# First block of experts listed ahead of the ranking, last two blocks added by one-hot products

## The chip, the cores and the metric

One core of one Trainium2 chip runs the whole program. The metric is the device time of one execution in microseconds (us). Before the change three runs gave a median of 2994.25 us (2991.94 to 2997.94).

## The reference, cut to what matters

Two transformer blocks run one after the other over 512 tokens, and 256 context tokens beside them in the first layer, all in float32 with a model width of 1024. The first block has two layers; each ends in a mixture of 32 experts of which every token takes two. This is the part that the change touches:

```python
def routed_experts(h, e_idx, e_w, w_gate, w_up, w_down):
    ...
    def expert_block(args):
        xblk, e = args
        return (jax.nn.silu(xblk @ w_gate[e]) * (xblk @ w_up[e])) @ w_down[e]

    yb = lax.map(expert_block, (xb, block_exp)).reshape(n_rows, d)
    return jnp.zeros((n_tok + 1, d), h.dtype).at[row_tok].add(yb * row_w[:, None])[:n_tok]

def hier_moe(h, grp_w, grp_b, exp_w, exp_b, w_gate, w_up, w_down):
    ...
    top_v, top_i = lax.top_k(e_logit, TOP_K)
    w = (g_prob * jax.nn.softmax(top_v, axis=-1)).astype(h.dtype)
    e_idx = g_idx[:, None] * EXPERTS_PER_GROUP + top_i.astype(jnp.int32)
    return routed_experts(h, e_idx, w, w_gate, w_up, w_down)
```

An expert has three matrices of 1024 by 512 floats (2 MB each), so each layer reads 201 MB of expert weights. Layer 0 routes 768 tokens, layer 1 routes 512. After layer 1 comes a final norm and the second block, whose first step is a feed-forward. With these inputs the experts 0 and 1 get 51 and 62 tokens in layer 0, 33 and 11 in layer 1.

## The kernel before

The activations X stay on chip, feature-major (8 tiles of 128 features by tokens). `moe` (L830) runs once per layer. It computes the router logits, writes the normalised tokens to a table `h2d` in DRAM (`token_major`), and then `router` (L607) picks two experts per token and gives each token its position within its expert. `places` (L663) ranks the 32 experts by load; two fixed experts (`FIRST`) always stand first, so that their weights can be loaded before the ranking is known. `order_list` (L700) writes the ranking to `pordi`; SyncE (SP) reads the expert numbers from it before it can issue the weights of any ranked expert. `slots` (L724) turns the places into lists, with one one-hot tile `sB` per 128 assignments on VectorE and one product each on TensorE: `stok` (which token sits in which row of which block), `srow` (the row of the result table) and `swt` (its weight).

The work then goes in blocks of 128 rows. A block is a single expert (the two fixed ones and the `MANY` most loaded ones: 8 in layer 0, 4 in layer 1) or a pair of lightly loaded experts with 64 rows each, which run in the two column halves of TensorE. There are 21 blocks in layer 0 and 19 in layer 1; the two fixed singles come first, then singles and pairs in turn, then pairs. `expert` (L1063) is a generator with four steps: transposes of the gathered rows, gate, up, down. For block e the program writes gate(e), the gather of block e+1 on GpSimd's queue, down(e-1) with the scatter of its weighted rows to the table `Yd` in DRAM, then up(e). Weights come through `raw` (L117) in pieces of 512 KB, 12 per expert, 384 per layer, in a ring of 24 buffers filled by SP's queue. The order of the instructions on each engine is made by a scheduler from the order of the program and its priorities.

The last block is not scattered. Its rows are added to X by products with a one-hot matrix `own` (L994 to L1012). All other rows come back from `Yd` by six (layer 0) or four (layer 1) reads `yr` of 1 MB on SP's queue, written in the program after the last block (L990); GpSimd adds the two rows of each token (L1020), TensorE transposes them (L1028, L1030), VectorE adds them to X (L1035 to L1041); squares and their sums for the next norm follow tile by tile (L1042 to L1055). In layer 1 the feed-forward (`ffn`, L1372) starts when these sums are there; `final_rows` (L1358) makes the row scales from them.

Among the rest of layer 1 are the s5 preparations (many small VectorE operations), which are spread beside the feed-forward.

Of the kernel before, what the change touches and what calls it, by code (L numbers as in the profile page):

```python
# [11 lines left out]
F32 = DT.float32  # L12
# [9 lines left out]
KD = 8  # L22
# [37 lines left out]
class Kernel:  # L60
    def __init__(self, tc, A):
        self.tc, self.nc, self.A = tc, tc.nc, A
        self.n = 0
        self.live = []
        self.fenced, self.behind, self.last_raw = 0, [], None
# [51 lines left out]
    def raw(self, src, queue=None):  # L117
# [9 lines left out]
        with ExitStack() as st:  # L127
            ins = self.behind.pop(0) if self.behind else None
            if ins:
                st.enter_context(self.tc.issue_after(ins))  # L130
# [180 lines left out]
    def open_x(self, ctx, n):  # L311
# [4 lines left out]
        self.rwc = p.tile([128, n, 36], F32, name="rwc")  # L316
        st.callback(s2.close)
# [283 lines left out]
    def router(self, l, lt, pool, p2, n_tok):  # L601
# [58 lines left out]
        V.tensor_copy(cnt, pc[:, :NE])  # L660
        self.choice = (oh, pos, v3, cnt)
        return self.places(l, p2, tt)

    def places(self, l, pool, tt):

        V = self.nc.vector
        oh, pos, _, cnt = self.choice
        mk = lambda name, *s, dt=F32: pool.tile([128, *s], dt, name="p" + name)
        n1 = FIRST[l] + MANY[l]
        nb = n1 + (NE - n1) // 2  # L670
# [17 lines left out]
        n = nb + nb % 2  # L688
        ohb = mk("ohb", tt, 2, n)
        V.tensor_tensor(ohb, self.iota[:, :n].unsqueeze(1).unsqueeze(1).to_broadcast([128, tt, 2, n]),  # L690
# [7 lines left out]
        return ohb, slot, nb  # L698

    def order_list(self, l, pool, p2):  # L700
# [12 lines left out]
        V.tensor_scalar(self.cap, self.cap, 128.0, None, op0=ALU.add)  # L713
# [10 lines left out]
    def slots(self, pool, rel, rhs, n_tok, name, bufs):  # L724
# [5 lines left out]
        n = rhs.shape[-1] // 3  # L730
        ps = self.bank()
        for t in range(tt):
            for j in range(2):
                B = pool.tile([128, 128], F32R, name=self.uid(name + "B"), tag=name + "B", bufs=bufs)
                V.tensor_scalar(B, self.iota, rel[:, t, j:j + 1], None, op0=ALU.is_equal)
                nc.tensor.matmul(ps[:, :3 * n], B, rhs[:, t, j], start=t == 0 and j == 0, stop=t == tt - 1 and j == 1)
# [3 lines left out]
        row = pool.tile([128, n], I32, name=name + "row")  # L740
        V.tensor_copy(row, f)
        tok = pool.tile([128, n], I32, name=name + "tok")
        V.tensor_scalar(tok, row, 1, None, op0=ALU.arith_shift_right)
        wt = pool.tile([128, n], F32, name=name + "wt")
# [32 lines left out]
    def overflow(self, l, n_tok, h2d, Yd, p2, x):  # L777
# [7 lines left out]
        with tc.If(nb > 0):  # L785
            with tc.For_i(0, nb, 1) as i:
                with ExitStack() as st:
# [25 lines left out]
                    row, tok, wt = self.slots(pool, rel, rhs, n_tok, "o", 2)  # L813
# [16 lines left out]
    def moe(self, l, n_tok, fg, side_work, stats):  # L830
# [8 lines left out]
        with ExitStack() as st:  # L839
# [4 lines left out]
            with ExitStack() as st1:  # L844
# [3 lines left out]
                with ExitStack() as st2:  # L848
# [36 lines left out]
                    for i in range(len(segs)):  # L885
                        for k in range(KD):
                            V.tensor_scalar(dg[:, k, i], self.ident, ga[:, k, i:i + 1], None, op0=ALU.mult)
                        for b in range(2):
# [5 lines left out]
                            nc.scalar.activation(sr[:, i, 512 * b:512 * b + 512], ps, AF.Copy)  # L894
                    put_back = []

                    def token_major():
                        for t in range(tt):
                            i = 0 if t < 4 else 1
                            for b in range(2):  # L900
# [6 lines left out]
                                if 2 * t + b < self.quick:  # L907
# [6 lines left out]
                    ohb, slot, nb = self.router(l, lt, pool, p2, n_tok)  # L914
                    v3 = self.choice[2]
                    n = ohb.shape[-1]
                    rhs = p2.tile([128, tt, 2, 3 * n], F32R, name="rhs", tag="lg")
                    for c in range(3):
                        V.tensor_tensor(rhs[:, :, :, n * c:n * c + n], ohb,
                                        v3[:, c].bitcast(F32).unsqueeze(3).to_broadcast([128, tt, 2, n]), ALU.mult)  # L920
                    row, tok, wt = self.slots(p2, slot, rhs, n_tok, "s", 2 * tt)
                    token_major()
                    self.behind = [None] * self.ahead[l] + put_back[1::2]
                    srow, stok, swt = [pool.tile([128, n], d, name=x) for x, d in (("srow", I32), ("stok", I32), ("swt", F32))]
                    for a, b in ((srow, row), (stok, tok), (swt, wt)):
                        V.tensor_copy(a, b)
                    self.order_list(l, pool, p2)

                n1 = FIRST[l] + MANY[l]
# [3 lines left out]
                ranks = lambda b: [b] if b < n1 else [2 * b - n1, 2 * b - n1 + 1]  # L933
                ysc = []
                with ExitStack() as st2:
# [26 lines left out]
                    for e in range(nb):  # L962
# [7 lines left out]
                        if e:  # L970
                            put(e - 1, self.rows_of(p2, next(ex[e - 1]), swt[:, turn[e - 1]:turn[e - 1] + 1]))
# [1262 lines left out]
```

## Time and profile before

| | us |
|---|---|
| median of 3 runs | 2994.25 |
| profiled execution, its own time | 2992.93 |
| its span in the trace | 2991.3 |
| experts of layer 0, first matmul to the scale of the next norm | 400.7 to 970.1 |
| experts of layer 1, first matmul to the feed-forward's third column block | 1324.9 to 1887.3 |

The span leaves 1.6 us of the execution's own time outside. TensorE is busy for 93% of the span, the DMA engines for between one and nine tenths of a slice, depending on the stage: in both expert stages they are at their limit for over 400 us. So the table by stretches, not the page's averages, tells which resource a stage waits for.

### The profile page before, as it was taken

The page shows a single profiled execution, that of the slowest core. Times are in us where ns is not written, and L with a number is a line of the kernel's source. Part 1 is how long each engine was busy: PE and PEld are TensorE (multiplying, and loading weights), DVE is VectorE, ACT ScalarE, POOL GpSimd, SP SyncE. Part 2 cuts the span into 40 slices and gives each one's busy share as a digit, 9 for nine tenths or more (in the row PEclk, how much of TensorE's full clock was granted, in tenths as well). Part 3 has the DMA queues.
Part 4 walks back from the last instruction along what each step waited for, and adds up shares of the span by engine and source line. Part 5 has one row for each costly group of instructions (what it writes and reads, how often), then busy time and mean ns, then how long its engine had stood idle before and what let it go on. Part 6 is the DMA issues. An engine that isn't in the chain of part 4 may idle for free.

```text
span 2991.3 us, 34947 instructions
## 1 busy us (share of the span) xinstructions
PE 2770.2 (93%) x12662; PEld 1815.0 (61%) x12662; DVE 1231.7 (41%) x2183; ACT 910.5 (30%) x1488; POOL 451.9 (15%) x430
## 2 busy tenths in 40 slices
PE   7989979998997999979999997999999889999998
PEld 3756734433433889844433333778888767888886
DVE  3883431000005566542000004954436777444335
ACT  3563201110102467511110002333225666323223
POOL 1662110000002000010100001371003140000000
PEclk9999989999998999989999998899999999999999
DMA  7558569999997211448999997343333422333331
GB/s 245 198 191 291 177 203 382 403 404 394 399 403 306 77 52 29 149 162 316 406 412 414 412 414 298 92 131 116 94 97 117 134 64 76 97 94 96 99 92 64
DMA packets 211426, 642.98 MB, mean 215 GB/s; under 512 B 32016, under 2 KB 41328, under 8 KB 209968
## 3 DMA queue, kind: packets, MB, share of 16 engines
q1 hardware_dynamic: 195648, 609.38, 56.2%
q0 software_dynamic: 15600, 31.32, 3.0%
q8 instruction: 101, 1.65, 0.2%
q14 instruction: 77, 0.63, 0.1%
HBM read 624.37 MB, written 37.19 MB: 221 GB/s over the span
## 4 chain that ended last, share of the span: by engine, by line
PE 62%; DMA 22%; DVE 9%; issue 4%; ACT 2%; SPq 1%; POOL 0%; DVEq 0%; POOLq 0%; ACTq 0%
PE ps L167 13%; PE ps L168 13%; PE ps L169 13%; PE ps L1089 9%; DMA raw<-exp_w_up 7%; DMA raw<-exp_w_down 6%; DMA raw<-exp_w_gate 6%; PE ps L1108 5%; PE ps L357 3%; DVE wl L90 1%; PE ps L1073 1%; DMA raw<-w_in_ab 1%; PE ps L219 1%; PE ps L1332 0%; DVE X L1035 0%
## 5 line engine op out<-in xcount | busy, mean ns | idle before, releaser
L1089 PE MATMUL ps<-raw,xt 128*64 128x512 f32 (+1 forms) x2048 | 635.6, 602 | 14.9 <-DMA raw<-exp_w_up 10.9
L167 PE MATMUL ps<-Hh,wh 128*128 128x512 f32 (+1 forms) x1320 | 495.5, 381 | 7.2 <-ACT Hh L260 2.1
L169 PE MATMUL ps<-Hh,wl 128*128 128x512 f32 (+1 forms) x1320 | 495.6, 377 | 6.4 <-DVE wl L90 6.3
L168 PE MATMUL ps<-Hl,wh 128*128 128x512 f32 (+1 forms) x1320 | 496.3, 377 | 1.6 <-DVE Hl L267 1.2
L1089 PEld LDWEIGHTS ps<-raw,xt 128*64 128x64 f32 (+1 forms) x2048 | 213.4, 150 | 389.6 <-issue 271.7
L88 ACT ACTIVATE wh<-raw 128x1024 fp32r<-128x1024 f32 (+1 forms) x224 | 231.5, 1039 | 559.8 <-PE ps L168 455.3
L90 DVE TENSOR_TENSOR wl<-raw,wh 128x1024 fp32r<-128x1024 f32 (+1 forms) x224 | 275.4, 1233 | 186.7 <-ACT wh L88 186.0
L1094 DVE TENSOR_TENSOR eh<-ps,eh 128x512 f32<-128x512 f32 x40 | 27.7, 692 | 753.7 <-PE ps L1089 704.8
L1108 PE MATMUL ps<-raw,ht 128*64 128x512 f32 (+1 forms) x1024 | 327.2, 603 | 2.3 <-issue 1.7
L167 PEld LDWEIGHTS ps<-Hh,wh 128*128 128x128 f32 x1320 | 248.9, 190 | 71.2 <-issue 5.6
L168 PEld LDWEIGHTS ps<-Hl,wh 128*128 128x128 f32 x1320 | 249.9, 189 | 52.5 <-issue 2.5
L169 PEld LDWEIGHTS ps<-Hh,wl 128*128 128x128 f32 x1320 | 249.1, 189 | 53.1 <-DVE wl L90 7.6
L1108 PEld LDWEIGHTS ps<-raw,ht 128*64 128x64 f32 (+1 forms) x1024 | 123.2, 150 | 192.7 <-issue 167.3
L1115 ACT ACTIVATE ey<-ps,swt 128x512 f32<-128x512 f32 x76 | 51.4, 686 | 323.8 <-PE ps L1108 305.3
L951 POOL DMA_INDIRECT yd<-ey,srow x38 | 37.9, 997 | 694.5 <-ACT ey L1115 579.5
L408 POOL TENSOR_TENSOR cg<-cg,cp 128x798 f32<-128x798 f32 x60 | 119.1, 1985 | 107.0 <-DVE cv L415 72.1
L1092 ACT ACTIVATE eh<-ps 128x512 f32<-128x512 f32 x40 | 23.9, 597 | 335.0 <-PE ps L1089 335.0
L1078 ACT ACTIVATE xt<-ps 128x512 f32<-128x512 f32 x40 | 23.9, 597 | 279.2 <-PE ps L1089 150.1
L357 PE MATMUL ps<-raw,sc 128*32 128x512 f32 x384 | 97.8, 614 | 3.5 <-DMA raw<-mod_w 3.5
L167 PE MATMUL ps<-Gh,wh 128*128 128x512 f32 x256 | 101.1, 395 | 0.0
L169 PE MATMUL ps<-Gh,wl 128*128 128x512 f32 x256 | 101.0, 395 | 0.0
L168 PE MATMUL ps<-Gl,wh 128*128 128x512 f32 x256 | 101.0, 395 | 0.0
(698 smaller groups left out, 3938.4 us busy)
## 6 DMA issues: line engine op xcount, KB each, us to landing
raw<-exp_w_up SPq DMA_DIRECT2D x256, 512.0 KB
raw<-exp_w_gate SPq DMA_DIRECT2D x256, 512.0 KB
raw<-exp_w_down SPq DMA_DIRECT2D x256, 512.0 KB
raw<-ffn_w SPq DMA_DIRECT2D x132, 512.0 KB
raw<-mod_w SPq DMA_DIRECT2D x96, 512.0 KB
yr<-yd SPq DMA_DIRECT2D x10, 1024.0 KB
X<-xT SPq DMA_DIRECT2D x16, 384.0 KB
raw<-w_in_ab SPq DMA_DIRECT2D x12, 512.0 KB
```

Source lines behind the costliest of these rows:

```text
L88: self.nc.scalar.activation(dst.hi, src, AF.Copy)
L90: self.split_last = eng.tensor_tensor(dst.lo, src, dst.hi.bitcast(F32), ALU.subtract).ins
L167: mm(ps, a.hi, b.hi, start=start, stop=False)
L168: mm(ps, a.hi, b.lo, start=False, stop=False)
L169: mm(ps, a.lo, b.hi, start=False, stop=stop)
L219: self.sums_last = self.nc.tensor.matmul(ps[:, t:t + 1], s, self.ones, start=True, stop=True).ins
L357: nc.tensor.matmul(ps[32 * g:32 * g + 32], self.sc[:, 2 * g + j, 30 - 2 * i:62 - 2 * i], w[:, j * 512:(j + 1) * 512], start=i == 0 and j = ...
L408: nc.gpsimd.tensor_tensor(a, a, t, ALU.add)
L951: ysc.append(nc.gpsimd.indirect_dma_start(out=Yd, out_offset=bass.IndirectOffsetOnAxis(ap=srow[:, b:b + 1], axis=0), in_=y, in_offset=None ...
L1089: mm(ps[s], XT[:, 2 * c + k, s], w[:, 512 * k:512 * k + 512], start=c == 0 and k == 0, stop=c == 3 and k == 1, **kw)
L1108: mm(pss[b][s], HT[:, k, s], w[:, 512 * b:512 * b + 512], start=k == 0, stop=k == 3, **kw)
L1115: self.nc.scalar.activation(y[:, 512 * b:512 * b + 512], pss[b], AF.Copy, scale=wt)
```

## The change

1. The first block is now a pair: the fixed experts 0 and 1 with 64 rows each. It has lists of its own (`fone`, `fplace`, `frhs`, `fB`, ending in `ftok`), which need only the positions and not the ranking. `places` is ordered behind them. The later blocks keep the list `s*` with the ranking. There are 20 blocks in layer 0 and 18 in layer 1, and a fixed expert's capacity falls from 128 to 64 rows (`light` in `order_list`); more would go through the overflow path.
2. Weights are issued strictly in the order of the program (`in_turn`).
3. The last two blocks are not scattered; zeros are scattered in their place at block 2. Both are added by one-hot products (`own_parts`, `add_own`).
4. The rows of all other blocks are read on GpSimd's queue, after the scatter of the third block from the end, into a ring of two buffers (`add_rows`); TensorE adds the two rows of a token while it transposes them. These steps are hooked into the last block's gate and up.
5. In layer 0 squares and sums are made per feature tile as the last block's adds finish. In layer 1 the last block's adds, squares and sums run inside the feed-forward's first two column blocks (`made`, `summed`), and `final_rows` follows them.
6. In layer 1 the shift of the norm is no longer added by GpSimd to the token table but by VectorE when the transposed rows are copied (`xshift`).

```diff
+                    one, place, none = [p2.tile([128, tt, 2], F32, name=x) for x in ("fone", "fplace", "fnone")]
+                    V.tensor_tensor(one, oh[:, :, :, 0], oh[:, :, :, 1], ALU.add)
+                    V.tensor_scalar(none, pos, 64.0, float(BIG), op0=ALU.is_ge, op1=ALU.mult)
+                    V.scalar_tensor_tensor(place, oh[:, :, :, 1], 64.0, pos, op0=ALU.mult, op1=ALU.add)
+                    V.tensor_tensor(place, place, none, ALU.add)
+                    first = lists("f", one.unsqueeze(3), place, 2 * tt)
                     token_major()
...
+                    with tc.issue_after(self.tok_last):
+                        placed = self.places(l, p2, tt)
+                    later = lists("s", *placed, 4)
                     self.order_list(l, pool, p2)
...
-                turn = list(range(FIRST[l]))
-                for i in range(nb - n1):
-                    turn += [FIRST[l] + i] * (i < MANY[l]) + [n1 + i]
+                turn = [0]
+                for i in range(nb - 1 - MANY[l]):
+                    turn += [1 + i] * (i < MANY[l]) + [1 + MANY[l] + i]
...
+                    def add_rows():
+
+                        Yv = Yd.rearrange("(t p j) d -> t p j d", p=128, j=2)
+                        ys = []
+                        for t in range(tt):
+                            ys.append(p2.tile([128, 2, D], F32, name=self.uid("yr"), tag="yr", bufs=2))
+                            nc.gpsimd.dma_start(ys[t], Yv[t])
+                        yield
+                        for t, y in enumerate(ys):
+                            for b in range(2):
+                                ps = self.bank("tp")
+                                for k in range(4):
+                                    f = slice(512 * b + 128 * k, 512 * b + 128 * k + 128)
+                                    for j in range(2):
+                                        nc.tensor.matmul(ps[:, 128 * k:128 * k + 128], y[:, j, f], self.ident, start=j == 0, stop=j == 1)
...
                         if e:
-                            put(e - 1, self.rows_of(p2, next(ex[e - 1]), swt[:, turn[e - 1]:turn[e - 1] + 1]))
+                            pss = next(ex[e - 1])
+                            if e == own[1]:
+                                o1 = p2.tile([128, n_tok], F32R, name="own", tag="own")
+                                self.hook = (3 if tt > 4 else 2, chain(rows, add_own(*own_parts(e - 1, pss, o1))))
+                            else:
+                                put(e - 1, self.rows_of(p2, pss, swt(turn[e - 1])))
...
+                    is_last = later_adds = len(segs) == 1
+                    o1 = self.own if later_adds else p2.tile([128, n_tok], F32R, name="own2", tag="own")
+                    adds = add_own(*own_parts(nb - 1, pss, o1))
...
+                    if later_adds:
+                        return adds
```

Three places show how the instructions now stand on their engines. On VectorE, in the router of layer 0, before (`pos` is the position within the expert, `pkey` to `prank` the ranking, `pordi` the order that SP reads):

```order
L658 TENSOR_REDUCE pos<-ox 128x12
L672 SCALAR_TENSOR_TENSOR pkey<-cnt,order_92 128x32
L674 TENSOR_TENSOR pgt<-pkey 128x1024
L675 TENSOR_REDUCE prank<-pgt 128x32
L677 TENSOR_TENSOR pox<-oh,prank 128x384
L704 TENSOR_TENSOR pgt<-prank,iota 128x1024
...
L710 CAST pordi<-pord 1x32
```

And with the change:

```order
L660 TENSOR_REDUCE pos<-ox 128x12
L948 TENSOR_SCALAR fnone<-pos 128x12
L949 SCALAR_TENSOR_TENSOR fplace<-oh,pos 128x12
L950 TENSOR_TENSOR fplace<-fplace,fnone 128x12
L740 TENSOR_SCALAR fB_2842<-iota,fplace 128x128
...
L748 TENSOR_SCALAR ftok<-frow 128x1
L670 COPY cnt<-ps_2810 128x32
L674 SCALAR_TENSOR_TENSOR pkey<-cnt,order_92 128x32
L676 TENSOR_TENSOR pgt<-pkey 128x1024
...
L713 CAST pordi<-pord 1x32
```

The first block's list, from `fnone` to `ftok`, now stands between the positions and the ranking.

On TensorE, at the start of the first block in layer 0, before (L736 are the list products, L1073 the transposes of the gathered rows `xg`, L1089 the first expert product):

```order
L736 MATMUL ps_2861<-rhs,sB_2895 128x66
L1073 MATMUL ps_3037<-ident,xg_2656 128x128 x4
L1073 MATMUL ps_3043<-ident,xg_2656 128x128 x4
L1089 MATMUL ps_3055<-raw_3056,xt_3036 128x512 x2
```

And with the change (L741, L1119 and L1138 are the same three):

```order
L741 MATMUL ps_2841<-frhs,fB_2875 128x4
L1119 MATMUL ps_3093<-ident,xg_2656 128x128 x4
L1119 MATMUL ps_3099<-ident,xg_2656 128x128 x4
L741 MATMUL ps_3024<-srhs,sB_3025 128x60
...
L741 MATMUL ps_3024<-srhs,sB_3058 128x60
L1138 MATMUL ps_3108<-raw_3109,xt_3092 64x512
```

The later list's twelve products stand ahead of the first expert product, as the twelve of the only list did before.

On TensorE, at the end of layer 0's experts, before (L1108 is down, L1089 gate and up, L1100 the transposes between, L1010 the one-hot adds):

```order
L1108 MATMUL ps_5541<-raw_5568,ht_5533 64x512
L1089 MATMUL ps_5580<-raw_5581,xt_5404 64x512
...
L1089 MATMUL ps_5580<-raw_5607,xt_5404 64x512
L1100 MATMUL ps_5615<-ident,eh_5498 128x128 x4
L1108 MATMUL ps_5621<-raw_5623,ht_5614 64x512
...
L1108 MATMUL ps_5622<-raw_5649,ht_5614 64x512
L1010 MATMUL ps_5684<-own,ysh_5672 128x512
```

And with the change (L1138 gate and up, L1029 the rows read back, L1150 the transposes, L1158 down), with further on the second piece:

```order
L1138 MATMUL ps_5536<-raw_5641,xt_5429 64x512
L1138 MATMUL ps_5725<-raw_5726,xt_5429 64x512
...
L1138 MATMUL ps_5725<-raw_5844,xt_5429 64x512
L1029 MATMUL ps_5545<-ident,yr_5523 128x128 x8
...
L1029 MATMUL ps_5660<-ident,yr_5529 128x128 x8
L1150 MATMUL ps_5675<-ident,eh_5385 128x128 x4
L1029 MATMUL ps_5734<-ident,yr_5531 128x128 x8
L1029 MATMUL ps_5747<-ident,yr_5531 128x128 x4
L1158 MATMUL ps_5681<-raw_5683,ht_5674 64x512
```

```order
L1158 MATMUL ps_5682<-raw_5709,ht_5674 64x512
L1029 MATMUL ps_5747<-ident,yr_5531 128x128 x4
L1029 MATMUL ps_5760<-ident,yr_5533 128x128 x8
L1029 MATMUL ps_5781<-ident,yr_5533 128x128 x8
L1010 MATMUL ps_5794<-own,ysh_5716 128x512
...
L1010 MATMUL ps_5870<-own,ysl_5717 128x256
L1150 MATMUL ps_5876<-ident,eh_5535 128x128 x4
L1158 MATMUL ps_5882<-raw_5884,ht_5875 64x512
```

Before, down of the last block but one stood ahead of up of the last block; now it stands behind it, between the row tiles, followed by its own adds and only then by the last block's down.

## Rows read from the trace of the kernel before

**Rows 1.** Page, the chain that ended last, shares of the span by engine
```profile
PE 62%; DMA 22%; DVE 9%; issue 4%; ACT 2%; SPq 1%; POOL 0%; DVEq 0%; POOLq 0%; ACTq 0%
```

**Rows 2.** Busy time by stretch: us, five engines' busy us, granted clock, DMA share, GB/s
```profile
394.00:470.00 76.00, 71.14 (x214) 33.59 (x216) 16.12 (x51) 9.20 (x14) 11.75 (x12) 0.94 0.75 251
500.00:900.00 400.00, 380.08 (x1387) 150.47 (x1386) 31.18 (x47) 39.35 (x62) 28.07 (x28) 0.99 1.02 401
922.00:932.00 10.00, 8.47 (x36) 3.58 (x36) 1.38 (x3) 0.61 (x1) 0.00 (x0) 1.00 0.60 224
1314.00:1390.00 76.00, 68.89 (x198) 33.25 (x200) 19.35 (x73) 8.01 (x12) 11.21 (x11) 0.91 0.73 239
1400.00:1800.00 400.00, 381.66 (x1408) 144.06 (x1406) 29.21 (x44) 37.01 (x58) 26.21 (x26) 0.99 1.02 412
```

**Rows 3.** Groups by shape, 470 to 900 us: count, busy us, mean ns, idle before
```profile
L1089 PE MATMUL ps<-raw,xt 128*64 128x512 f32 x640 | 162.4, 600 | 5.0 <-DMA raw<-exp_w_up 3.2 <-DMA raw<-exp_w_gate 1.2 <-PEq L785 0.4
L1089 PE MATMUL ps<-raw,xt 128*128 128x512 f32 x224 | 99.7, 596 | 0.0
```

**Rows 4.** Timeline of SP, layer 0: start us, us, operation
```profile
387.42 2.03 SPq L131 DMA_DIRECT2D raw<-exp_w_gate  x4
```

**Rows 5.** Timeline of all engines, layer 1
```profile
1313.49 1.95 SPq L131 DMA_DIRECT2D raw<-exp_w_gate  x4
```

**Rows 6.** Timeline of DVE, router of layer 0
```profile
389.45 2.44 DVE L735 TENSOR_SCALAR sB<-iota,pslot 128x128 fp32r<-128x128 f32 x12
393.24 0.18 DVE L743 TENSOR_SCALAR stok<-srow 128x22 int32<-128x22 int32 x1
```

**Rows 7.** Timeline of DVE, router of layer 1
```profile
1298.42 1.19 DVE L577 SCALAR_TENSOR_TENSOR at<-at,iota 128x32 f32<-128x32 f32 x1
1302.61 0.19 DVE L577 SCALAR_TENSOR_TENSOR bt<-bt,iota 128x32 f32<-128x32 f32 x1
```

**Rows 8.** Timeline of DVE, end of the experts in layer 0
```profile
921.94 0.69 DVE L1094 TENSOR_TENSOR eh<-ps,eh 128x512 f32<-128x512 f32 x1 [29.80 <-PE ps L1089]
933.44 2.22 DVE L1005 TENSOR_SCALAR own<-toks,tokf 128x768 fp32r<-128x768 f32 x1
937.03 3.53 DVE L1012 SCALAR_TENSOR_TENSOR X<-ps,mod,X 128x512 f32<-128x512 f32 x6 [1.38 <-PE ps L1010]
942.97 1.38 DVE L1035 SCALAR_TENSOR_TENSOR X<-ps,mod,X 128x128 f32<-128x128 f32 x5
967.66 1.22 DVE L90 TENSOR_TENSOR wl<-raw,wh 128x1024 fp32r<-128x1024 f32 x1
970.08 0.16 DVE L229 TENSOR_SCALAR nv<-sums 128x6 f32<-128x6 f32 x1
```

**Rows 9.** Timeline of PE, the last down product in layer 0
```profile
924.26 7.73 PE L1108 MATMUL ps<-raw,ht 128*64 128x512 f32 x32 [0.83 <-issue]
```

**Rows 10.** Timeline of all engines, the rows read back in layer 0
```profile
927.91 5.38 SPq L991 DMA_DIRECT2D yr<-yd  x6
932.90 2.34 POOL L1020 TENSOR_TENSOR yr<-yr 128x1024 f32<-128x1024 f32 x1 [19.13 <-DMA yr<-yd]
```

**Rows 11.** Timeline of PE, end of the experts in layer 1
```profile
1827.88 0.75 PE L1100 MATMUL ps<-ident,eh 128*128 128x128 f32 x4 [0.86 <-DVE eh L1094]
1829.46 8.80 PE L1108 MATMUL ps<-raw,ht 128*64 128x512 f32 x32 [0.83 <-issue]
...
1887.29 0.47 PE L167 MATMUL ps<-Hh,wh 128*128 128x512 f32 x1
```

**Rows 12.** Timeline of DVE, ahead of the feed-forward
```profile
1873.25 0.15 DVE L229 TENSOR_SCALAR nv<-sums 128x4 f32<-128x4 f32 x1
1881.50 0.16 DVE L1366 TENSOR_TENSOR nq<-nq,nq 128x4 f32<-128x4 f32 x1 [0.15 <-POOL nq L231]
1882.62 0.18 DVE L1497 TENSOR_TENSOR x<-par,dtp 128x16 f32<-128x16 f32 x1
1886.31 0.18 DVE L1453 TENSOR_SCALAR exp<-exp 128x32 f32<-128x32 f32 x1
```

More of the change, by code (lines that the diff above doesn't have):

```diff
@@ L316, in open_x @@
         self.rwc = p.tile([128, n, 36], F32, name="rwc")
+        self.own = p.tile([128, L], F32R, name="own") if n == 1 else None
         st.callback(s2.close)
@@ L957, in moe @@
+                    own = range(nb - 2, nb)
+                    is_last = False
+                    rows = add_rows()
                     start(0)
@@ L975, in moe @@
                                 self.extra(pool)
+                            z = p2.tile([128, 2, D], F32, name="zero", tag="yr", bufs=2)[:, 0]
+                            nc.gpsimd.memset(z, 0.0)
+                            for i in own:
+                                put(i, z)
                         if e == self.pause:
@@ new lines, in moe @@
+                    if later_adds:
+                        return adds
+                    sums = self.bank()
+                    for k in adds:
+                        x2 = p2.tile([128, 2, D], F32, name=self.uid("x2"), tag="yr", bufs=2)[:, 0, :n_tok]
+                        a = nc.scalar.activation(x2, X[:, k, :n_tok], AF.Square)
+                        for t in range(tt):
+                            nc.tensor.matmul(sums[:, KD * t + k:KD * t + k + 1], x2[:, 128 * t:128 * t + 128], self.ones, start=True, stop=True)
@@ L1058, in ew, with hooked @@
+                    self.tail = [a.ins]
+                    self.fence()
+                    s = self.cst.tile([128, 1, tt], F32, name=self.uid("sums"))
+                    V.tensor_reduce(s[:, 0], sums[:, :tt * KD].rearrange("p (t k) -> p t k", k=KD), axis=AX.X, op=ALU.add)
+        return s
+    hook = None
+    def hooked(self):
+        if self.hook:
+            for _ in range(self.hook[0]):
+                next(self.hook[1], None)
     def ew(self, name, l, e):
@@ L1368, in final_rows, with ffn @@
         self.rows(dst, r1)
-    def ffn(self, g, w13, w2, sums=None):
+    def ffn(self, g, w13, w2, adds=None):
         tc, nc, A, X = self.tc, self.nc, self.A, self.X
@@ L1410, in ffn @@
             W = self.blocks(A[w13])
-            self.linear(W, H, KD, range(2), [(0, L)], evac, lead=2, prek=prek)
-            if sums is not None:
+            self.linear(W, H, KD, range(2), [(0, L)], evac, lead=2, prek=prek, each=each)
+            if adds is not None:
                 with ExitStack() as s1:
```

253 lines of the change are left out of this document (129 added, 124 removed).

## Prediction

> **What bounds the kernel now.** I read the chain that ended last first: TensorE holds 62% of it and DMA 22% [rows 1]. These are shares of a span with many stages, so the table by stretches comes next [rows 2]. In both expert stages the DMA engines are full for 400 us at a time (share 1.02, 401 GB/s in layer 0, 412 GB/s in layer 1): there the weights set the pace. The reader should see the exception beside it: the first 76 us of each stage move only 251 and 239 GB/s. The reason is in the groups by shape [rows 3]. A single expert's matmul takes 99.7/224 = 0.445 us, so its 48 take 21.4 us, while its 6.29 MB need 15.7 us at 401 GB/s: two singles in a row are bound by TensorE. A pair's 96 matmuls at 162.4/640 = 0.254 us take 24.4 us for 12.6 MB that need 31.4 us: bound by DMA. At the stage's end the stream runs dry (224 GB/s from 922 us on) and a serial tail follows, on VectorE above all. So the change has four terms: two streams and two tails.
>
> **Streams, layer 0.** SP issues the first ranked weights at 387.42 us [rows 4], when the order is known. The new list stands ahead of the ranking on VectorE. The old list's part from `sB` to `stok` takes 389.45 to 393.42 us, 4.0 us [rows 6]; with six small operations more, the two masks and the weights' products, I take 5.7 us. So SP comes at 393.1 us, later than now, and the first expert product gains little, since TensorE still has the later list's products ahead of it. The gain is behind that: the pair frees buffers faster than they fill, so I let the stream run at 401 GB/s from 394.1 us. It has to move 368 pieces (only 16 instead of 20 are loaded beforehand, the pair's gate and up) of 0.524 MB, 192.9 MB; 1536 rows of 4 KB in and out, 12.6 MB; and the first two row tiles, 2.1 MB. Of this about 1.2 MB land after the last up product (2.2 MB moved from 922 to 932 us [rows 2], 1 MB of it a row tile). 206.4 MB take 514.7 us, so the last up product ends at 908.8 us, not 921.94 [rows 8]: **-13.1 us**. Those two tiles are on GpSimd's otherwise idle queue, but the engines are full, so they cost 5.2 us of this. If that queue brought bandwidth of its own, the term would be -18.3.
>
> **Streams, layer 1.** The list costs less (eight one-hot tiles, 4.3 us), and GpSimd no longer adds the shift. While it did, VectorE's small operations stretched: 1.19 us for one that takes 0.19 us a little later [rows 7]. Four such give back 3.2 us. SP comes 1.1 us later than 1313.49 [rows 5]. 192.9 + 8.4 + 2.1 - 1.2 = 202.2 MB at 412 GB/s take 490.8 us, ending at 1806.4 instead of 1827.0 us (the transposes' start less their wait [rows 11]): **-20.6 us**.
>
> **Tail, layer 0.** From the last up product to `nv`, the scale of the next norm, the kernel now takes 970.08 - 921.94 = 48.1 us [rows 8]. With the change both TensorE and VectorE have the row tiles behind that product. Times from it: gate multiply 0.7; a step of four adds 1.1 us (1.38 for five [rows 8]) plus a hand-off, 1.2, so tiles 0 and 1, long read, end at 5.6. The ring has two buffers: tile 2's read starts at 3.0, when tile 0 is transposed. The nearest row is the first read now, issued at 927.91 and used at 932.90, 5.0 us [rows 10], so tile 2 lands at 8, tile 3 at 10.5, and their steps end at 13. Transposed `h` 0.9; tile 4 lands at 15.5, one step; then down of the last block but one, 7.7 us [rows 9], which before lay hidden in the stream: 24.5. Its split and the last three steps end at 29.3. Sixteen adds of 0.59 us (3.53 for six) end at 39, a second `own` (2.2) and `h` at 42.5, the last down at 50.2, split and first products at 53, sixteen adds at 62.4, three weight splits of 1.22 us that stand ahead of the sums at 66.1, `nv` at 66.5. What goes is the reductions of the squares and GpSimd's additions; what comes is the second down and the second set of adds. **+18.4 us**. Between 15 (reads never waited for) and 28 (down at the 8.8 us of layer 1 [rows 11], hand-offs of 1 us more at each of eight places).
>
> **Tail, layer 1.** Now 1887.29 - 1827.02 = 60.3 us to the feed-forward's third column block [rows 11]. With the change, in the same way: row steps 13; down 14.5 to 22.7; eight adds to 31.4; the last down 32.8 to 41. Behind that VectorE has, in its order, the split with two weight splits (4.4), eight adds and eight splits of 0.7 (11), some 65 small s5 operations at 0.11 us (33 between 1882.62 and 1886.31 [rows 12]) to 0.2 where each needs the one before, taken as 8.5, and one weight split (1.2): 66.1. The scale chain now takes 1873.25 to 1881.5 us, 8.25 [rows 12]; third block at 74.4. **+14.1 us**, between 10 (s5 operations in the gaps) and 21. The first two column blocks' matmuls hide beside VectorE; the chain itself was hidden beside them before and is bare now, since TensorE has the scale's transposes ahead of the third block.
>
> **Small edits.** Zeros, the token numbers and the issue order lie in the stream, beside 24.4 us of TensorE work per pair; without that cover the two zero scatters would cost what the two real ones did, so nothing. VectorE's copies in place of ScalarE's in layer 1 have room (29 of 400 us busy [rows 2]).
>
> **Sum.** -13.1 - 20.6 + 18.4 + 14.1 = -1.2 us. From the profiled execution's 2992.93 us, which is 1.3 below the median of the runs, this gives **2991.7 us**. A run of this kernel can tell 0.2%, 6 us, from no change, so the forecast is no measurable difference: early gains given back late.
>
> **Rivals.**
>
> *Fuller streams, faster.* If gaps in layer 0's stream close and it runs at layer 1's 412 GB/s, 206.4 MB take 501.0 us, 13.7 less; with the low bounds of the tails (3.4 and 4.1 less) 2970.5, with half of that 2981. For it: the 5.0 us that TensorE waits for weights between 470 and 900 us [rows 3] show that it isn't what holds the stream. Against: layer 0 moves more scattered rows in the same time, and they stay.
>
> *The two-buffer ring, slower.* If a row tile takes 10 us instead of 5 from issue to use, tiles 2 and 3 come 5 us later in each layer and tile 4 another 5 us: +10 in layer 0, +5 in layer 1, 3006.7. It decides from 6.5 us a read on, where tile 4 comes after the steps ahead of it. For it: in the full stream a 0.5 MB gather waits for its share like every weight, and these reads come while the last weights land. Against: after the last up product little is left to land (224 GB/s [rows 2]). The Trainium skill ("DMA: Bandwidth & Descriptors", section "Bandwidth", the table of transfers issued from GpSimd) gives 6.15 us of DMA time for 1 MB and, in the section on one DMA, about 2 us fixed; taken together as an estimate, 8 us a read, the sum would be some 9 us higher, 3001. No run here shows a read of this size from GpSimd's queue; the 5.0 us row is one of SP.
>
> *Stream not filled at the start, slower.* If the first pair leaves the ring as empty as the two singles did, half of both stream terms goes: +17, 3008.6. Against: the pair's matmul time per MB is 24.4/12.6, the single's 21.4/6.3.
>
> *The change doesn't do what it says.* More than 64 tokens for a fixed expert would add an overflow block, some 16 us of weights and its matmuls, 3015. The counts 51, 62, 33 and 11 speak against it.
>
> **How the numbers follow.** Forecast 0.47, within 2983 to 3001 (same 0.36, faster 0.10, slower 0.01); fuller streams 0.25, faster; the ring 0.16, an empty start 0.09 and an overflow block 0.03, all three slower but for 0.01 that ends within 0.2%. Faster 0.35, same 0.37, slower 0.28. The range runs from 2976 to 3007: it takes in half of the fast case's reach and the ring's price, and leaves out the ends.
>
> **What would show it.** In the trace after: SP's first ranked weights near 393 and 1314.6 us; over 380 GB/s from 395 us on; the last up products near 909 and, on the shifted clock, 21 us earlier in layer 1; reads of 5 us between rounds of row steps; down of the last block but one behind them; tails of 66 and 74 us. I am wrong if the stream starts with a hole, if the tails grow by less than 10 us each, or if TensorE waits over 5 us for a row tile.

## The result, and the profile after

The changed kernel takes 3029.3 us (median of 4 runs, 3019.7 to 3030.7); the kernel before, run beside it on the same chip, 2995.9. The ratio is 1.0106, 95% interval 1.0082 to 1.0130: **slower by about 33 us**, where I forecast no difference and a range that ended at 3007. The profiled execution is the fastest of the four (3019.7, span 3018.1). So the marks below, which are read within profiles, account for the 26.8 us between the two profiled spans and not for all of the 33.

Seven marks, the begin and the end among them, cut the program into stretches whose differences add up to that of the spans. "Logits" is the start of VectorE's `lt`, "last up" that of the last `eh`, "third block" the feed-forward's third column block. The last two columns are experiments that are told below.

| stretch, us | before | after | difference | forecast | new start alone | new tail in layer 1 only |
|---|---|---|---|---|---|---|
| begin to layer 0's logits | 360.1 | 355.6 | -4.5 | 0 | 357.0 | 356.9 |
| logits to last up, layer 0 | 561.9 | 546.9 | -15.0 | -13.1 | 542.9 | 543.1 |
| last up to `nv`, layer 0 | 48.1 | 83.4 | **+35.2** | +18.4 | 47.5 | 49.0 |
| `nv` to last up, layer 1 | 857.0 | 851.6 | **-5.5** | -20.6 | 848.8 | 853.6 |
| last up to third block, layer 1 | 60.2 | 76.5 | +16.3 | +14.1 | 59.0 | 80.4 |
| third block to the end | 1104.0 | 1104.2 | +0.2 | 0 | 1102.1 | 1105.9 |

So two of my four terms came out near their forecast, and two failed: layer 0's tail by 17 us and layer 1's stream by 15. The -4.5 us at the top is no gain to rely on: the profiles of the experiments come there between 355.7 and 359.8 us, whichever edit they hold; why the kernel before is the last of all stays open.

The table by stretches of the changed kernel (us, busy us of PE, PEld, DVE, ACT and POOL, granted clock, DMA share, GB/s) answers to [rows 2]; its last two lines are the end of layer 0:

```profile
394.00:470.00 76.00, 74.08 (x286) 31.27 (x284) 16.97 (x54) 8.70 (x13) 12.40 (x12) 0.99 1.02 402
500.00:900.00 400.00, 369.72 (x1295) 144.73 (x1292) 28.43 (x43) 35.99 (x57) 25.24 (x26) 0.97 1.02 402
1314.00:1390.00 76.00, 62.28 (x282) 33.12 (x281) 32.72 (x125) 8.77 (x14) 13.04 (x13) 0.87 0.85 324
1400.00:1800.00 400.00, 381.54 (x1377) 141.61 (x1374) 35.33 (x56) 27.28 (x42) 25.47 (x26) 0.99 1.02 404
...
957.80:965.00 7.20, 6.56 (x43) 5.35 (x42) 5.76 (x10) 3.25 (x5) 2.13 (x4) 1.00 0.30 113
965.00:985.80 20.80, 19.67 (x88) 18.92 (x87) 8.45 (x13) 7.02 (x8) 2.20 (x5) 0.51 0.23 81
```

The hole at the stream's start is closed in layer 0: 402 GB/s from 394 us on, where it was 251. Layer 1's first window begins here 20 us ahead of SP's issue, because the whole layer comes later; from 1354 to 1430 us it moves 399 GB/s, so its hole is closed too. Layer 1 ran at 412 GB/s between 1400 and 1800 us before and runs at 404 now. SP's first ranked weights [rows 4, 5] come here:

```profile
387.47 1.96 SPq L132 DMA_DIRECT2D raw<-exp_w_gate  x4
...
1333.87 1.95 SPq L132 DMA_DIRECT2D raw<-exp_w_gate  x4
```

The end of layer 0 on TensorE (start, us, line, operation, count; the idle time before it and its cause in brackets):

```profile
902.29 7.41 PE L1029 MATMUL ps<-ident,yr 128*128 128x128 f32 x64
914.72 8.83 PE L1029 MATMUL ps<-ident,yr 128*128 128x128 f32 x64 [5.02 <-DMA yr<-yd]
...
928.25 7.09 PE L1158 MATMUL ps<-raw,ht 128*64 128x512 f32 x32
935.27 4.73 PE L1029 MATMUL ps<-ident,yr 128*128 128x128 f32 x40
...
950.75 7.09 PE L1158 MATMUL ps<-raw,ht 128*64 128x512 f32 x32 [1.43 <-DVE ht L1151]
...
961.46 1.39 PE L1090 MATMUL ps<-ones,x 128*128 128x1 f32 x12
...
968.89 2.55 PE L1090 MATMUL ps<-ones,x 128*128 128x1 f32 x12
...
979.55 5.11 PE L1090 MATMUL ps<-ones,x 128*128 128x1 f32 x24
```

and on VectorE, which answers to [rows 8]:

```profile
902.46 0.69 DVE L1144 TENSOR_TENSOR eh<-ps,eh 128x512 f32<-128x512 f32 x1 [35.66 <-PE ps L1138]
904.38 1.13 DVE L1032 SCALAR_TENSOR_TENSOR X<-ps,mod,X 128x128 f32<-128x128 f32 x4 [1.22 <-PE ps L1029]
906.16 1.13 DVE L1032 SCALAR_TENSOR_TENSOR X<-ps,mod,X 128x128 f32<-128x128 f32 x4 [0.66 <-PE ps L1029]
...
918.23 1.12 DVE L1032 SCALAR_TENSOR_TENSOR X<-ps,mod,X 128x128 f32<-128x128 f32 x4 [7.37 <-PE ps L1029]
...
941.08 8.48 DVE L1012 SCALAR_TENSOR_TENSOR X<-ps,mod,X 128x512 f32<-128x512 f32 x16
949.49 0.61 DVE L1001 TENSOR_SCALAR own<-acc,tokf 128x768 fp32r<-128x768 f32 x1
...
979.79 0.48 DVE L1012 SCALAR_TENSOR_TENSOR X<-ps,mod,X 128x256 f32<-128x256 f32 x1 [2.24 <-PE ps L1010]
982.19 3.50 DVE L90 TENSOR_TENSOR wl<-raw,wh 128x1024 fp32r<-128x1024 f32 x3 [1.92 <-ACT wh L88]
985.84 0.17 DVE L230 TENSOR_SCALAR nv<-sums 128x6 f32<-128x6 f32 x1
```

The reader should see three things. VectorE waits 0.66 us for TensorE in most row steps, so a step takes 1.79 us. The third row tile holds TensorE up for 5.02 us. And from 957.8 us on, behind the last down product, 28 us go by until `nv`.

SP's queue shows a fourth. In the kernel before, twelve loads of weights were ordered behind the reads of the rows (`self.behind = 12 * [self.rows_read]`, L992), so the next stage's weights `w_in_cd` came after them. The change drops this edge, and they now go out 4.7 us ahead of the third read. Before and after:

```profile
933.34 65.64 SPq L131 DMA_DIRECT2D raw<-w_in_cd  x10
```

```profile
901.74 84.31 SPq L132 DMA_DIRECT2D raw<-w_in_cd  x8
```

From the issue of that read to its use, 906.4 to 914.7 us, the DMA engines are full (share 1.03, 419 GB/s).

### The profile page after: what moved, and what is told of

Same layout as the page of the kernel before. It is cut to its first block, busy times and chain, and to the rows that moved or that the text cites. A ratio compares the mean times of both kernels' runs of the same rounds, so it can differ in the third digit from the quotient of the medians.

```text
span 3018.1 us, 35760 instructions
## 1 busy us (share of the span) xinstructions
PE 2804.3 (93%) x13046; PEld 1850.7 (61%) x13046; DVE 1234.4 (41%) x2272; ACT 883.0 (29%) x1416; POOL 430.7 (14%) x428
## 5 line engine op out<-in xcount | busy, mean ns | idle before, releaser
L1138 PE MATMUL ps<-raw,xt 128*64 128x512 f32 (+1 forms) x2048 | 627.1, 614 | 46.3 <-DMA raw<-exp_w_up 32.9
L1138 PEld LDWEIGHTS ps<-raw,xt 128*64 128x64 f32 (+1 forms) x2048 | 208.8, 149 | 415.7 <-issue 279.3
L1158 PE MATMUL ps<-raw,ht 128*64 128x512 f32 (+1 forms) x1024 | 308.2, 599 | 4.7 <-DVE ht L1151 4.0
L1158 PEld LDWEIGHTS ps<-raw,ht 128*64 128x64 f32 (+1 forms) x1024 | 113.1, 146 | 186.6 <-issue 163.0
L1165 ACT ACTIVATE ey<-ps,swt 128x512 f32<-128x512 f32 x64 | 43.0, 686 | 237.6 <-PE ps L1158 235.2
L982 POOL DMA_INDIRECT yd<-ey,srow x32 | 31.9, 996 | 553.0 <-ACT ey L1165 500.2
L1482 DVE TENSOR_TENSOR fs<-ps,fs 128x512 f32<-128x512 f32 x44 | 30.4, 691 | 135.8 <-PE ps L170 135.1
```

Of the source, the lines that this page charges most:

```text
L982: ysc.append(nc.gpsimd.indirect_dma_start(out=Yd, out_offset=bass.IndirectOffsetOnAxis(ap=srow(turn[e]), axis=0), in_=y, in_offset=None, b ...
L1138: mm(ps[s], XT[:, 2 * c + k, s], w[:, 512 * k:512 * k + 512], start=c == 0 and k == 0, stop=c == 3 and k == 1, **kw)
L1158: mm(pss[b][s], HT[:, k, s], w[:, 512 * b:512 * b + 512], start=k == 0, stop=k == 3, **kw)
L1165: self.nc.scalar.activation(y[:, 512 * b:512 * b + 512], pss[b], AF.Copy, scale=wt)
L1482: V.tensor_tensor(s, ps, s, ALU.mult)
```

## Experiments

My theory after reading this: the new start is worth what the forecast gave it, and the new tails lose it. In layer 0 three things lie on the path: waits for reads, row steps at TensorE's pace, and 48 products of one column for the sums. Rivals: the start gave little, or the waits alone make the difference.

**The new start alone.** The kernel before with the first pair, its list, the order of the loads and the shift (parts 1, 2 and 6); the last block alone is added by one-hot products, and rows are read at the end, as before.

Against the changed kernel:

```diff
-                                self.hook = (2, rows)
...
-                            for i in own:
-                                put(i, z)
+                            put(nb - 1, z)
...
-                    adds = add_own(*own_parts(nb - 1, pss, o1))
...
+            for t in range(tt):
+                self.rows_read = nc.sync.dma_start(yr[t], Yv[t]).ins
```

> The changed start alone (pair of fixed experts with a list of its own, weights in program order, shift added at the transposed copy), with the end of the kernel before: one block added by products, all other rows read back after it, squares and sums per row tile. Theory 'the start gains, the ends lose': the last up product of layer 0 comes 19 us earlier than in the kernel before as it does in the changed kernel, layer 1's start loses 8 us to the ranking behind the first list and to the shift's products and its stream gains 10, the ends are as before: about 2976 us. Rival 'the early last up product is only bought by later down weights' (some 4 MB still land behind it): layer 0 gains under 10 us and layer 1 nothing, about 2986 us or more.

Measured 2961.6 us, ratio to before 0.9886 (0.9869 to 0.9902): 35.6 us faster. Both expectations fall: the gain is 14 us larger than even the theory says (2976). The stream starts full in both layers:

```profile
394.00:470.00 76.00, 75.91 (x290) 32.24 (x291) 17.84 (x58) 8.81 (x13) 11.36 (x11) 0.96 1.02 398
...
1314.00:1390.00 76.00, 76.00 (x286) 32.34 (x283) 17.71 (x53) 7.69 (x11) 8.08 (x8) 1.00 1.02 402
```

By the marks the old tails behind it keep their lengths (47.5 and 59.0 us). So the start gains 36 us and the tails lose 68. Of the gain 19.0 us lie in layer 0 and only 8.2 in layer 1; the rest lies before, between and behind them. The forecast's two stream terms add up to 33.7, but as -13.1 and -20.6: that the sums are close is chance.

**Which tail.** The changed kernel, with the old tail in layer 0.

```diff
+                    new = len(segs) == 1
                     own = range(nb - 2, nb)
...
-                            if e == own[1]:
+                            if new and e == own[1]:
...
+            for t in range(tt):
+                self.rows_read = nc.sync.dma_start(yr[t], Yv[t]).ins
```

> The changed kernel, but layer 0 ends with the old tail (last block alone by one-hot products, rows read at the end, sums per row tile); layer 1 keeps the new one. Theory: by the ledger of the marks layer 1's new tail costs 17.5 us behind its last up product (76.5 against 59.0 with the new start alone) and its reads in the stream 7.0 us (503.6 against 496.7), so 2961.6 + 24.5 = 2986; layer 0's part (35.9 + 4.7) is gone from the changed kernel's 3029.3, which gives 2989. Rival: the two tails share a cost (the s5 operations and the feed-forward's weights that come behind), and layer 1's alone is nearly free, since its adds lie beside the feed-forward's first two column blocks: 2962 to 2972.

Measured 2991.5 us (0.9984, 0.9975 to 0.9994), close to the theory's 2989: layer 1's tail costs 29.9 us behind the new start, and layer 0's the other 37.9. The rival falls: adds beside the feed-forward aren't free. By the marks 21.4 of layer 1's lie behind the last up product, 4.8 between `nv` and it, and 3.8 behind the third block.

**Reads.** Only two of the row tiles are read and used again and again, so most tokens get wrong rows.

```diff
-                        for t in range(tt):
+                        for t in range(2):
...
-                        for t, y in enumerate(ys):
+                        for t, y in enumerate(ys * (tt // 2)):
```

> The changed kernel with only the first two row tiles read back (their data are added for the later tiles too, so four of six and two of four reads of 1 MB are left out). Theory 'two-buffer ring': TensorE's waits for row tiles (5.0 us in layer 0, 3.5 in layer 1, and the slower steps behind them) go, 10 to 14 us less, about 3017 us. Rival 'order': the waits are a small part, the step is bound by TensorE and by what stands behind the last up product: under 6 us less, 3024 us or more.

Measured 3016.1 us (1.0065, 1.0048 to 1.0082), 13 below the changed kernel by the medians. The steps then run on without a gap:

```profile
905.79 14.56 PE L1029 MATMUL ps<-ident,yr 128*128 128x128 f32 x128
```

Layer 0's tail falls from 83.4 to 77.9 us, layer 1's is no shorter (77.6). So the waits are worth 5.5 us by the marks; the rest of the 13 is no more than the 11 us over which the changed kernel's own runs spread. By its total the theory holds, by the marks the rival's size. The last down product ends 8.3 us earlier behind the last up product (47.1 instead of 55.4), but the stretch from there to `nv` takes 30.8 us instead of 28.0. The eight steps at TensorE's own pace, 14.56/8 = 1.82 us, are left.

**Row steps.** Of the two products that add a token's two rows only the first is issued, so the second row is left out.

```diff
-                                    for j in range(2):
-                                        nc.tensor.matmul(ps[:, 128 * k:128 * k + 128], y[:, j, f], self.ident, start=j == 0, stop=j == 1)
+                                    nc.tensor.matmul(ps[:, 128 * k:128 * k + 128], y[:, 0, f], self.ident, start=True, stop=True)
```

> The changed kernel, but of the two products by which TensorE adds the two rows of a token while it transposes them only the first is issued: the second row of each token is left out of the sum, the reads and VectorE's additions stay. Theory: a row step is bound by its products (sixteen records of 0.116 us, 1.8 us a step) and VectorE needs 1.13; with half of them a step falls to 1.2 us. In layer 0 twelve steps, of which those behind the waits for reads hide their part: 4 to 7 us gained there, and 0 to 3 in layer 1: 3020 to 3025. Rival: the steps are held by the reads alone (13 us went when only two tiles were read), so faster steps only wait longer: 3027 to 3030.

Measured 3019.6 us (1.0079, 1.0062 to 1.0096). Four steps now take 3.84 us instead of 7.41, but the next read is then waited for longer, and the four steps behind it meet a granted clock of 0.50 (914.8 to 921.5 us):

```profile
906.48 3.84 PE L1028 MATMUL ps<-ident,yr 128*128 128x128 f32 x32
917.23 6.06 PE L1028 MATMUL ps<-ident,yr 128*128 128x128 f32 x32 [6.91 <-DMA yr<-yd]
```

Layer 0's tail is 76.0 us, 7.4 shorter; layer 1's is no shorter. Theory and rival each hold in part: products and reads are two limits close to each other, and taking one away runs into the other.

**Sums.** 42 of the 48 small products of layer 0's sums are left out, so the next norm's sum holds one of eight feature tiles.

```diff
-                        for t in range(tt):
+                        for t in range(tt if k == KD - 1 else 0):
                             nc.tensor.matmul(sums[:, KD * t + k:KD * t + k + 1], x2[:, 128 * t:128 * t + 128], self.ones, start=True, stop=True)
...
-                    V.tensor_reduce(s[:, 0], sums[:, :tt * KD].rearrange("p (t k) -> p t k", k=KD), axis=AX.X, op=ALU.add)
+                    V.tensor_copy(s[:, 0], sums[:, KD - 1:tt * KD:KD])
```

> The changed kernel with layer 0's sums of squares made from the last feature tile alone: 42 of 48 products with a column of ones are left out. Theory 'sums on TensorE': the last adds take 12 us instead of 27, about 14 us less, 3015 us. Rival 'clock': TensorE is slow there for what came before, and VectorE's 8.5 us of adds set the pace anyway: under 5 us less, 3025 us or more.

Measured 3012.7 us (1.0056, 1.0040 to 1.0073), 16.6 less, as the theory says; layer 0's tail is 70.4 us, 13.0 shorter. The sixteen adds, which were done at 980.3 and began at 957.8 us (22.5), now take 9 us:

```profile
960.52 0.85 PE L1010 MATMUL ps<-own,ysh 128*128 128x512 f32 x3
...
969.32 0.28 PE L1010 MATMUL ps<-own,ysl 128*128 128x256 f32 x1
971.48 2.59 PE L1090 MATMUL ps<-ones,x 128*128 128x1 f32 x12 [1.88 <-ACT x L1088]
```

**Down ahead.** TensorE's last up product is ordered behind down of the last block but one, so that rows and that down move into the stream.

```diff
-                        next(ex[e])
+                        with ExitStack() as st3:
+                            if e == own[1]:
+                                st3.enter_context(tc.issue_after(self.down_last))
+                            next(ex[e])
...
-                    mm(pss[b][s], HT[:, k, s], w[:, 512 * b:512 * b + 512], start=k == 0, stop=k == 3, **kw)
+                    self.down_last = mm(pss[b][s], HT[:, k, s], w[:, 512 * b:512 * b + 512], start=k == 0, stop=k == 3, **kw).ins
```

> The changed kernel with one edge in TensorE's order: the last block's up product stands behind down of the block before it, so that row tiles, that down and most of its adds lie in the stream ahead of the last up product. Theory 'order': some 35 us of layer 0's end and 20 us of layer 1's move under the stream, about 2980 us, below the kernel before. Rival 'TensorE blocks the stream': reads of row tiles in the full stream hold TensorE and thereby the weights' buffers, so that the last up product comes later by most of it: 3010 us or more.

Measured 3004.6 us (1.0028, 1.0015 to 1.0040), 24.8 less: half of what the theory says (2980), and less than the rival's 3010. The last up product comes 27 us later, but logits to `nv` takes 616.2 instead of 630.3 us. TensorE now waits for a read while weights stream:

```profile
895.09 10.24 PE L1029 MATMUL ps<-ident,yr 128*128 128x128 f32 x64 [5.00 <-DMA yr<-yd]
```

**Both.** The last two edits at once.

> The changed kernel with two of the earlier edits at once: the last up product ordered behind the down product of the last block but one, and 42 of the 48 small products of layer 0's sums of squares left out (the next norm's scale is then wrong in size). Theory: the two causes are separate, the waits ahead of the second down product and the products behind the last one, and their gains add: 3029.3 - 24.8 - 16.6 = 2988, within 2984 to 2992. Rival: they overlap, since with the rows done early the sums were no longer last: 2996 to 3005. In either case the new tail stays 20 us or more above the old one behind the same start (2961.6).

Measured 2989.1 us (0.9977, 0.9968 to 0.9987): the gains add. From logits to `nv` the kernel takes 605.7 us, 24.5 less than the changed kernel, against 14.1 and 11.7 for each edit alone. The old tail behind the same start still needs 15 us less (590.4).

**The shift.** In the new start alone, layer 1's sixteen 1x1 products behind the logits.

```diff
...
+                        with tc.issue_after(lg_last):
-                        for k in range(KD):
-                            nc.tensor.matmul(ps[:, k:k + 1], sr[0:1, 0, k:D:KD], self.ones[0:1], start=True, stop=True)
+                            for k in range(KD):
+                                nc.tensor.matmul(ps[:, k:k + 1], sr[0:1, 0, k:D:KD], self.ones[0:1], start=True, stop=True)
```

> The new start with the old tail once more, but in layer 1 the sixteen 1x1 products that turn the norm's shift (xshift) are ordered behind the logits' product instead of ahead of it. Theory: these 3.96 us stand on TensorE between the norm's sums and the logits, so the router of layer 1 and all behind it come 3 to 4 us earlier than with the new start alone (2961.6): 2958. Rival: the router's VectorE chain is held by GpSimd and its own work, not by this product, or the time is given back in the stream because its end is set by bytes from SP's first ranked issue on, whose list waits for GpSimd: 2961 to 2962, no gain.

Measured **2956.6 us** (0.9872, 0.9856 to 0.9889), 5 us less by the medians and 4 by the ratios to the kernel before, as the theory says. By the marks the logits come 5.8 us earlier behind layer 0's `nv` and the last up product 2.4 us: part is given back, since `pos` now comes 12.4 us behind the logits instead of 9.4. The products of 3.96 us stood ahead of the logits in the changed kernel:

```profile
1305.77 3.96 PE L907 MATMUL ps<-ones,sr 1*128 1x1 f32 x16
1309.65 3.23 PE L918 MATMUL ps<-dg,X 128*128 128x128 f32 x16
1312.67 1.47 PE L880 MATMUL ps<-rsel,lg 128*128 128x36 f32 x8
```

and stand behind them in this one:

```profile
1270.44 1.08 PE L878 MATMUL ps<-rsel,lg 128*128 128x36 f32 x8 [1.48 <-ACT lg L875]
1271.46 3.96 PE L906 MATMUL ps<-ones,sr 1*128 1x1 f32 x16
```

**The order of the loads.** The new start alone, without `in_turn`.

```diff
-                    self.in_turn = True
```

> The new start with the old tail, without the strict order of the weight loads (in_turn is never set). Theory: the pair and its early list make the stream full from its beginning, and the order of the loads is worth only the 4 to 5 us by which the modulation of the first mixer, and with it the router of layer 0, came earlier: 2966. Rival: the strict order is what closes the hole at the stream's start (weights land in the order in which TensorE asks for them): without it half of the 35.6 us goes, 2979 or more.

Measured 2960.4 us (0.9884, 0.9868 to 0.9901). Both expectations fall. Layer 0's stream does start slower without the order (366 GB/s from 394 to 470 us, 398 with it), but from SP's first ranked issue to the last up product it takes 511.2 us instead of 510.3. So the order is worth nothing that these runs can tell, and no more with the late shift:

> The new start with the old tail, the shift's products behind the logits, and no strict order of the loads. Theory: the order of the loads was worth nothing measurable (2960.4 without it, 2961.6 with it), so 2955 to 2958, the same as with it (2956.6). Rival: with the router of layer 1 4 us earlier a late weight shows, and the order is worth something: over 2960.

Measured 2956.7 us (0.9869, 0.9853 to 0.9886), so the first expectation holds here.

**The list.** The pair stays, but its list is made behind the ranking.

```diff
+                    placed = self.places(l, p2, tt)
                     self.order_list(l, pool, p2)
+                    with tc.issue_after(self.order_last):
...
+                        first = lists("f", one.unsqueeze(3), place, 2 * tt)
...
-                    with tc.issue_after(self.tok_last):
-                        placed = self.places(l, p2, tt)
```

> The new start with the old tail and the late shift (2956.6), but the first block's list (fone to ftok) is written behind the ranking and the order for SP, so only the pair is left of the new start. Theory: SP comes 5 us earlier in each layer, yet the first pair's rows come some 12 us later and no buffer is free until its gate has run: the ring is full after eight more loads (4.2 MB, 10 us), and the stream then stands for about 14 us in each layer: about 9 us lost per layer, 2970 to 2980. So the list, not only the pair, is what fills the stream's start. Rival: the pair alone does it, since it frees buffers faster than they fill once it runs: 2950 to 2958.

Measured 2963.3 us (0.9890, 0.9874 to 0.9907), 6.7 more than with the early list (4.4 by the marks from logits to last up in layer 0, 3.8 from `nv` to last up in layer 1). Both expectations miss. Most of the gain stays without the early list, so the pair makes it, with the shift on VectorE, which no run takes away. SP comes 27.5 us behind layer 0's logits instead of 32.5, but the first rows come at 397.3 us instead of 388.3, and the stream starts at 356 GB/s where the new start alone gave 398:

```profile
394.00:470.00 76.00, 72.66 (x270) 31.23 (x271) 15.78 (x51) 8.53 (x13) 9.08 (x9) 0.95 0.94 356
```

```profile
397.34 1.94 PE L1106 MATMUL ps<-ident,xg 128*128 128x128 f32 x8 [4.02 <-DMA xg<-h2d,ftok]
```

## Why the prediction was wrong

My sum was -1.2 us, and the marks say +26.8. Two steps make the difference: layer 0's tail, 16.8 us over its forecast, and layer 1's stream, 15.1 us short of it. The 4.5 us that the program gained ahead of layer 0's logits I hadn't forecast.

**Streams, layer 0: right.** I let the stream run at 401 GB/s for 514.7 us, which is 515.7 from SP's first ranked issue to the last up product; it takes 902.46 - 387.47 = 515.0 us. The list costs SP 4.6 us from the logits on (31.9 instead of 27.3), where I took 5.7. The reads are in the stream as I priced them: without them, in the new start alone, it takes 510.3.

**Streams, layer 1: the failed term of the early gain**, -20.6 forecast, -5.5 measured. The larger step is the rate: the 490.8 us of stream were worked out at 412 GB/s, the kernel before's rate, and it ran at 404; 202.2 MB at 404 GB/s are 500.5, nearly 10 us more, and from SP's issue on it takes 503.6 where I had 491.8. Why layer 1 ran faster before isn't settled. It is neither the new tail nor the order of the loads: from 1400 to 1780 us the new start alone runs at 405 GB/s, and without the order at 404. Then I counted GpSimd's shift as 3.2 us saved on VectorE, which came (10.9 us from logits to `pos` before, 7.7 after), but not its replacement: the sixteen products ahead of the logits, 4.1 us from `nv` to `lt`. Moving them gave 4 to 5 us in the new start.

**Tail, layer 0: the failed term of the late loss**, +18.4 forecast, +35.2 measured. Times from the last up product:

| step | forecast | measured |
|---|---|---|
| tiles 0 and 1 added | 5.6 | 8.4 |
| tiles 2 and 3 added | 13 | 22.3 |
| down of the last block but one | 24.5 | 32.9 |
| remaining row steps | 29.3 | 38.7 |
| its sixteen adds | 39 | 47.1 |
| last down | 50.2 | 55.4 |
| `nv` | 66.5 | 83.4 |

Three steps failed. (1) A row step was priced by VectorE at 1.2 us; it takes 1.79, because TensorE's eight products of 128 by 128 are sixteen records of 0.116 us (the trace holds two for each product); with half of them left out TensorE needs 0.96. (2) A read was priced by SP's 5.0 us [rows 10], on the premise that little is left to land behind the last up product. GpSimd's queue issues the third at 906.42 and TensorE uses it at 914.72, 8.3 us later, with the engines full at 419 GB/s of the next stage's weights and the rows. In layer 1, where SP issues no weights from 1836 to 1873 us and the engines move 264 GB/s, the same read takes 6.7 us, 1841.40 to 1848.12. No run takes these weights away alone, so their share of the wait is argued and not shown. The page gives the median from issue to landing:

```profile
yr<-yd POOLq DMA_DIRECT2D x10, 1024.0 KB, 8.2
```

By the Trainium skill ("DMA: Bandwidth & Descriptors", section "Bandwidth", and for the fixed part the section "Anatomy of one DMA") my estimate was 8 us a read. The 8.3 us of layer 0 and the median agree in size and layer 1's 6.7 does not; with other traffic on the engines neither shows the page's two parts. It isn't GpSimd's queue as such either: SP's reads of this size, several in flight, have medians of 8.5 us (the late shift) to 8.9 (the late list). The two-buffer rival, which decides from 6.5 us on, was right in mechanism; I gave it 0.16. (3) From the last down to `nv` I took 16.3 us, and it takes 28.0. I priced the adds and three weight splits and put the sums' products at nothing. They are 96 records between the adds on TensorE and take 17.9 us, where before VectorE's reductions left one product per row tile. Leaving 42 of the 48 products out gave 13.0 us back. Against these, `own` and the hand-off to the last down took 1.2 us together instead of 3.5.

**Tail, layer 1: right in size, in part by luck**: by the marks +16.3 against +14.1, inside its bounds of 10 and 21. The last down is done 41.6 us behind the last up product, where I took 41, but the steps to it were wrong against each other: the row steps end at 19.2 us instead of 13, for the same two reasons as in layer 0, and shorter products and adds bring 5.6 us of it back. TensorE waits for a read there too, 3.46 us:

```profile
1848.12 7.38 PE L1029 MATMUL ps<-ident,yr 128*128 128x128 f32 x64 [3.46 <-DMA yr<-yd]
```

Measured alone it costs more, 29.9 us. By its marks 21.4 lie in the stretch of the forecast, just over its upper bound; 4.8 lie ahead of the last up product, about what I had put into the stream for two reads (2.1 MB at 412 GB/s, 5.1 us); and 3.8 lie behind the third block, where I had put nothing.

**One of the three signs that I had named as proof against me** came: TensorE waits over 5 us for a row tile. The rival on fuller streams fell: layer 0's stream stays at 402 GB/s; the 19 us that the new start alone gains there are the hole at its beginning, and the reads that it doesn't hold. An overflow block did not come.

## What to carry to other kernels

A change that edits a stage's start and its end should be cut in two before it is judged: here one half gains 36 us and the other loses 68. Price each moved step by the slowest of the engines it runs on, counting TensorE's records and not its instructions. Price a read by what else will be on the DMA engines, and ask what a dropped order had held back. Work that moves to another engine has to be priced there too: the sums went from VectorE's reductions to many one-column products between TensorE's adds, and 13 us hang on them.

## What the runs showed of the hardware

A product with one column costs as much as one with 128: 0.116 us a record at a granted clock of 1.00 (twelve records of 128x1 in 1.39 us, 64 of 128x128 in 7.41).

The clock falls while the sums' products stand between the adds. From 957.8 to 965 us it is 1.00; from 965 to 985.8 us, where a third group of these products begins, it is 0.51, near the lower of the two levels (1.2 GHz), though TensorE is busy for 19.67 of 20.8 us, and twelve records take 2.55 us instead of 1.39. All 96 take 17.9 us; at 0.116 us a record they would take 11.1, an estimate. The run with two reads shows the same: 0.50 from 957.7 us on, 1.1 us behind the start of the first group, with TensorE busy for 24.94 of 26.1 us. With 42 of the products left out the clock stays at 1.00 through all of the adds (960.5 to 969.6 us) and is 0.50 only behind them (971.7 to 975.4 us). So leaving the products out saves their own time and that of the lower clock together, and the runs don't part the two. Why the clock falls there isn't settled by these runs.
